# Where the last gate block gets its sigmoid: stored as exp(-x) and finished on two engines, or stored raw and finished on ScalarE

## The chip, the cores and the metric

The kernel runs on one core of one Trainium2 chip. The metric is the device time of one execution in microseconds (us). The engines of the core are TensorE (PE, with its weight loads PEld), VectorE (DVE), ScalarE (ACT), GpSimd (POOL) and SyncE (SP, which here only issues DMAs). Each engine takes its own instructions in a fixed order and waits, at the head of its queue, for whatever its next instruction needs.

## The reference

The reference is one decoder block on an input of 1024 tokens by 1024 channels, in float32. One projection gives pooling input p, queries, keys and values of four differential attention heads, and two gates of 1024 channels each. What matters here is how the two branches are merged:

```python
ya = einsum('bsc,cd->bsd', pool_mixer(p, pool_mix, pool_scale), w_branch_a)
yb = einsum('bsc,cd->bsd', diff_attention(q, k, v, ...), w_branch_b)
m = sigmoid(gate_a) * ya + sigmoid(gate_b) * yb
h = h + rms_norm(einsum('bsd,de->bse', m, w_out), mix_post_g)
```

A SwiGLU feed-forward layer follows, with silu of one product times another.

## The kernel before, in words

All activations lie in transposed form, channels on the 128 partitions and tokens along the free dimension. 1024 channels are eight blocks d of 128; 1024 tokens are two halves t of 512. A matrix product in float32 precision is made of three products of high and low parts (`triple`, lines 246 to 248); a high part is a cast on ACT, a low part a subtraction on DVE (`sub`, line 87).

The input projection runs in units. A unit computes two blocks of output columns for all tokens by a scheme of seven products (`seven_steps`). The eight gate units d = 0 to 7 compute block d of both gates; `gate_done` (line 622) is called for each finished quarter, writes it through ACT into a staging tile `g_st`, and stores the tile to DRAM (`sgd`). For d = 0 to 6 the ACT instruction is the sigmoid (line 629). The last unit, d = 7, isn't run with the others: it is kept as a generator and serves as the first part of the filler of the attention stage. For it, line 627 stores exp(-x).

The attention stage is a loop over 32 pairs of head and query block. For each pair there are scores on PE, a bias and row minimum on DVE (L771), Exp on ACT (L774), a combination of the two softmaxes on POOL (L778 to L781), transposes on PE (L797) with a cast on ACT (L799) and a subtraction on DVE to the operands `AT`, and value products on PE (L811). Between these steps PE works on a filler: the rest of the last gate unit, and then `branch(0, ...)`, the first branch (pooling output times `w_branch_a`). `PACES` says how many filler steps are written into the program for each attention step. When attention is over, `branch(1, ...)` does the second branch (attention output times `w_branch_b`), and the output projection follows, whose operands (`out_operands`) take the merged blocks in the order 0 to 7.

Both branches are one function, `branch` (line 705). It goes through 16 groups, a block d and a token half t each, of twelve matmuls (four `triple`s). `fetch` loads the weights of two blocks, four groups at a time. `gate(n)` loads the gate of group n by a DMA on SP's queue into one of two buffers for that half (named `p` for t = 0 and `sg` for t = 1 in the profile); it is called two groups ahead. `take` multiplies the group's PSUM result by the gate on DVE (`ma` in the first branch; `m` in the second, where `ma` is then added). PSUM has two banks for branch groups (`fil`), so a group needs the `take` of the group before last.

For d = 7 `gate` also finishes the sigmoid from exp(-x): POOL takes the minimum with 1e37 and adds 1 (line 726), DVE takes the reciprocal (line 727). The blocks are done in the order of line 703,

```python
BLOCKS = (0, 1, 2, 3, 6, 7, 4, 5)
```

so block 7 is groups 10 and 11 of 16 in each branch.

The framework keeps the dependencies and puts the semaphores. Outside the parts marked as manual schedule, which the attention and branch stages are not, it also decides the order of each engine's queue, from the program's order and from what it holds to be ready. On ACT a function needs its table: the compiler puts an ACT_TABLE_LOAD where the next function isn't in the table that is loaded. Copies, casts and squares have run here under each of the tables without a load.

Of the kernel before, what the change touches and what calls it, by code (L numbers as in the profile page):

```python
# [12 lines left out]
AF = mybir.ActivationFunctionType  # L13
ALU = mybir.AluOpType
# [5 lines left out]
KD = D // P  # L20
# [19 lines left out]
def block_kernel(ctx, tc, x, w_in, pool_mix, pool_scale, w_branch_a, lam_q1, lam_k1, lam_q2,  # L40
                 lam_k2, subln_g, w_branch_b, w_out, mix_pre_g, mix_post_g, ffn_pre_g, ffn_post_g,
                 w_ffn_gate, w_ffn_up, w_ffn_down, out):
    nc = tc.nc
# [24 lines left out]
    def b4(shape, dt, s):  # L68
        return sb.tile(shape, dt, tag="b4", bufs=B4, name=name(s))
# [4 lines left out]
    def fil(s):  # L74
        return ps.tile([P, HALF], F32, tag="fil", bufs=2, name=name(s))
# [13 lines left out]
    def load_w(src, k, n, s, pool=False):  # L89

        raw = wp.tile([P, k, n], F32, tag="wraw", bufs=2, name=name(s + "_raw"))
        hi = wp.tile([P, k, n], F32R, tag="whi", bufs=2, name=name(s + "_hi"))
        lo = wp.tile([P, k, n], F32R, tag="wlo", bufs=2, name=name(s + "_lo"))
        nc.sync.dma_start(raw, src.rearrange("(k p) n -> p k n", p=P))
        nc.scalar.copy(hi, raw)
        if pool:
            nc.gpsimd.tensor_tensor(out=lo, in0=raw, in1=f32(hi), op=ALU.subtract)  # L97
        else:
            sub(lo, raw, hi)
        return hi, lo  # L100
# [143 lines left out]
    def triple(o, ah, al, bh, bl, start, stop, goes_on):  # L244

        nc.tensor.matmul(o, ah, bh, start=start, stop=False, skip_group_check=goes_on)  # L246
        nc.tensor.matmul(o, ah, bl, start=False, stop=False, skip_group_check=goes_on)  # L247
        nc.tensor.matmul(o, al, bh, start=False, stop=stop, skip_group_check=goes_on)  # L248
# [12 lines left out]
    def temp(s):  # L261
        if s in ("p1", "p5", "c11"):
            return sm.tile([P, HALF], F32, tag="ft", bufs=2, name=name(s))
        return sm.tile([P, HALF], F32, tag="sg", bufs=2, name=name(s))
# [45 lines left out]
    def half(t):  # L310
        return slice(t * HALF, (t + 1) * HALF)
# [101 lines left out]
    def take(tb):  # L413
        for kq in range(2):
            nc.scalar.copy(U[f"A{tb // 4 + 1}{kq + 1}"][0][:, :, token_cols(tb)], turned[tb][kq])
            nc.scalar.copy(raw_cols(tb, kq), turned[tb][kq])
# [46 lines left out]
    with tc.manual_schedule(engines={nc.tensor.engine, nc.scalar.engine, nc.vector.engine, nc.gpsimd.engine}):  # L463
# [79 lines left out]
        for i in range(2):  # L543
            nc.vector.tensor_tensor_reduce(out=lams_at[:, 4, :], in0=lams_at[:, 2 * i, :], in1=lams_at[:, 2 * i + 1, :],
                                           scale=1.0, scalar=0.0, op0=ALU.mult, op1=ALU.add,
# [76 lines left out]
    def gate_done(d):  # L622
        st, seen = [b4([P, S], F32, "g_st") for _ in range(2)], [0, 0]

        def done(e, t, src):
            if d == KD - 1:
                nc.scalar.activation(st[e][:, half(t)], src, AF.Exp, scale=-1.0)
            else:
                nc.scalar.activation(st[e][:, half(t)], src, AF.Sigmoid)
            seen[e] += 1  # L630
            if seen[e] == 2:
                nc.scalar.dma_start(sgd[e][d], st[e])
        return done
# [66 lines left out]
            return src[k // 2][0][:, k % 2, half(t)], src[k // 2][1][:, k % 2, half(t)]  # L700
        return mov

    BLOCKS = (0, 1, 2, 3, 6, 7, 4, 5)

    def branch(e, w, mov, take):

        order = [(d, t) for d in BLOCKS for t in range(2)]
        if e == 1:
            order[:4] = [(0, 1), (1, 1), (0, 0), (1, 0)]
        ws, gates = {}, {}  # L710

        def fetch(n):
            if 2 * n < KD:
                d = BLOCKS[2 * n]
                hi, lo = load_w(w[:, d * P:(d + 2) * P], 4, 2 * P, "wb", e == 0)
                for i in range(2):
                    c = slice(i * P, (i + 1) * P)
                    ws[d + i] = hi[:, :, c], lo[:, :, c]

        def gate(n):  # L720
            if n < len(order):
                d, t = order[n]
                sg = gates[d, t] = temp(("p1", "sg")[t])
                nc.sync.dma_start(sg, sgd[e][d][:, half(t)])
                if d == KD - 1:
                    nc.gpsimd.tensor_scalar(sg, sg, 1.0e37, 1.0, op0=ALU.min, op1=ALU.add)
                    nc.vector.reciprocal(sg, sg)

        fetch(0)
        gate(0)  # L730
        gate(1)
        for n, (d, t) in enumerate(order):
            if n % 4 == 0:
                fetch(n // 4 + 1)
            gate(n + 2)
            bh, bl = ws[d]
            o = fil("branch")
            for k in range(4):
                triple(o, bh[:, k, :], bl[:, k, :], *mov(t, k), k == 0, k == 3, False)
                yield  # L740
            take(d, t, o, gates.pop((d, t)))
# [110 lines left out]
    def filling():  # L852
        yield from last_unit
        for i in range(2):
            y2.append((a8([P, 2, S], F32R, "y2h"), a8([P, 2, S], F32R, "y2l")))
            for j in range(2):
                for t, s in zip(y2[i], range(2)):
                    nc.sync.dma_start(f32(t[:, j, :]), yd[2 * i + j][:, s, :])
        ma.extend([[a8([P, 4, HALF], F32, "ma") for _ in range(KD // 4)] for _ in range(2)])
        for _ in load_head(1):  # L860
            pass
        yield from branch(0, w_branch_a, quad_mov(y2), take_a)
# [56 lines left out]
    for _ in branch(1, w_branch_b, quad_mov(OT), take_b):  # L919
        pass  # L920
# [130 lines left out]
    with tc.manual_schedule(engines={nc.tensor.engine, nc.scalar.engine, nc.vector.engine, nc.gpsimd.engine}):  # L1051
# [43 lines left out]
        for c in (c0, c1):  # L1095
            nc.vector.scalar_tensor_tensor(out=xr[:, c], in0=og[:, c], scalar=r[:, 0:1], in1=xr[:, c],
                                           op0=ALU.mult, op1=ALU.add)
# [8 lines left out]
        for c in (c0, c1):  # L1106
            nc.vector.scalar_tensor_tensor(out=og[:, c], in0=xr[:, c], scalar=r[:, 1:2], in1=gpre[:, c],
                                           op0=ALU.mult, op1=ALU.mult)
        sg = temp("sg")
# [22 lines left out]
    sg = temp("sg")  # L1132
# [185 lines left out]
```

## Time and profile before

| | us |
|---|---|
| median of 3 runs | 1276.46 |
| lowest and highest | 1275.58, 1278.18 |
| the profiled execution | 1275.52 |
| its span, first to last instruction | 1273.7 |
| last gate unit's four Exp stores (L627) | 342.8 to 354.9 |
| first branch's products with gates (`ma`) | 372.4 to 489.3 |
| second branch's products with gates (`m`) | 492.7 to 538.8 |
| table loads on ACT, four in all, each | 1.283 |

The mean granted clock of PE is 0.995 of full speed. The times in the profile's rows are microseconds from the start of the span. A row of the timeline has start, duration, engine, line, operation, output<-input and shapes, and in brackets how long the engine stood idle just before and what ended that. A row of the waits has who waited for whom, the sum, the number of waits and the longest. A row of the groups has the count, the busy sum, the mean duration in ns, and the idle time before. Matmul rows overlap: a matmul of 512 columns shows 0.39 us, but the next starts about 0.23 us later.

### The profile page before, as it was taken

Reading aid. Unit: us, or ns where it says so; the run is one execution under the profiler, and the core shown is the slowest. Engines: PE = TensorE matmul, PEld = TensorE weight load, DVE = VectorE, ACT = ScalarE, POOL = GpSimd, SP = SyncE. Lnnn points to the kernel's source line nnn. Section 1 sums busy time; section 2 is a strip of 40 time slices with the busy share of each in tenths; the row PEclk is TensorE's granted clock in tenths of the full one; section 3 lists DMA queues with packets and bytes.
Section 4 is the critical chain, followed back from the end, with each engine's and each line's share of the span. In section 5 each row is a group of like instructions: output and inputs, shape, how many; then the busy total and the mean of one; then the engine's idle time right before and its main releaser. Section 6 shows DMA issues by size and latency. Waiting matters only on the chain.

```text
span 1273.7 us, 15951 instructions
## 1 busy us (share of the span) xinstructions
PE 1244.2 (98%) x5952; PEld 1039.9 (82%) x5952; DVE 834.6 (66%) x1217; ACT 566.6 (44%) x1021; POOL 235.6 (18%) x241
## 2 busy tenths in 40 slices
PE   6999999999999899999999999999999999999997
PEld 6988778888888797788878888888888888888886
DVE  6884775435467786856699556556656537965666
ACT  7452344434567572234564333333333334454542
POOL 1000000000478871101102121022122011000221
PEclk9999999999999999999999999999999999999999
DMA  8263346234698113533315232233332358733235
GB/s 280 84 203 118 135 151 217 96 103 149 244 262 254 59 50 108 182 131 134 99 58 157 99 108 92 92 107 124 104 103 91 116 195 285 248 91 107 81 103 207
DMA packets 135566, 179.18 MB, mean 141 GB/s; under 512 B 7872, under 2 KB 90304, under 8 KB 133056
## 3 DMA queue, kind: packets, MB, share of 16 engines
q1 hardware_dynamic: 123552, 146.56, 36.8%
q10 hardware_dynamic: 11936, 31.60, 6.6%
q8 instruction: 47, 0.77, 0.3%
q14 instruction: 31, 0.25, 0.1%
HBM read 124.39 MB, written 53.74 MB: 140 GB/s over the span
## 4 chain that ended last, share of the span: by engine, by line
PE 86%; DVE 5%; ACT 3%; issue 3%; POOL 2%; DMA 1%; ACTq 0%; POOLq 0%; DVEq 0%; SPq 0%
PE Y L246 10%; PE Y L248 10%; PE Y L247 10%; PE X L246 5%; PE X L247 5%; PE X L248 5%; PE Yd L247 3%; PE Yd L248 3%; PE Yd L246 3%; PE Z L248 2%; PE Z L247 2%; PE Z L246 2%; PE o L811 2%; PE wo L972 2%; PE wo L970 2%
## 5 line engine op out<-in xcount | busy, mean ns | idle before, releaser
L164 DVE TENSOR_TENSOR p<-Z,p 128x512 f32<-128x512 f32 x35 | 24.2, 690 | 156.2 <-PE Z L248 154.5
L247 PE MATMUL Y<-A_lo,Wh 128*128 128x512 f32 x296 | 115.7, 391 | 0.3 <-DVE A_lo L87 0.3
L248 PE MATMUL Y<-A_hi,Wl 128*128 128x512 f32 x296 | 115.3, 390 | 0.1
L246 PE MATMUL Y<-A_hi,Wh 128*128 128x512 f32 x296 | 115.3, 390 | 0.0
L246 PE MATMUL Y<-S_hi,Wh 128*128 128x512 f32 x280 | 109.3, 390 | 0.0
L247 PE MATMUL Y<-S_lo,Wh 128*128 128x512 f32 x280 | 109.2, 390 | 0.0
L248 PE MATMUL Y<-S_hi,Wl 128*128 128x512 f32 x280 | 109.1, 390 | 0.0
L207 ACT CAST Wh<-wf_t 128x1024 fp32r<-128x1024 f32 x70 | 72.8, 1053 | 61.5 <-PE X L248 35.5
L87 DVE TENSOR_TENSOR Wl<-wf_t,Wh 128x1024 fp32r<-128x1024 f32 x70 | 86.9, 1248 | 13.9 <-PE Y L247 9.3
L87 DVE TENSOR_TENSOR w_op<-wd,w_op 128x512 fp32r<-128x512 f32 x77 | 56.3, 731 | 52.7 <-ACT w_op L168 52.7
L168 ACT CAST w_op<-wd 128x512 fp32r<-128x512 f32 x77 | 47.9, 622 | 73.7 <-PE Yd L248 31.6
L164 DVE TENSOR_TENSOR wf_t<-w_raw,wf_t 128x512 f32<-128x512 f32 x70 | 75.6, 1081 | 1.0
L247 PE MATMUL Yd<-w_op,s_op 128*128 128x512 f32 x176 | 68.7, 390 | 0.2 <-DVE w_op L87 0.2
L246 PE MATMUL Yd<-w_op,s_op 128*128 128x512 f32 x176 | 68.6, 390 | 0.0
L248 PE MATMUL Yd<-w_op,s_op 128*128 128x512 f32 x176 | 68.3, 389 | 0.0
L248 PEld LDWEIGHTS Y<-A_hi,Wl 128*128 128x128 f32 x296 | 55.6, 188 | 11.9 <-DVE Wl L87 0.5
L247 PEld LDWEIGHTS Y<-A_lo,Wh 128*128 128x128 f32 x296 | 55.6, 188 | 11.9 <-DVE A_lo L87 0.7
L246 PEld LDWEIGHTS Y<-A_hi,Wh 128*128 128x128 f32 x296 | 55.6, 188 | 11.6 <-ACT Wh L207 0.2
L97 POOL TENSOR_TENSOR wb_lo<-wb_raw,wb_hi 128x1024 fp32r<-128x1024 f32 x4 | 10.5, 2631 | 291.8 <-DVE Wl L87 291.8
L168 ACT CAST s_op<-s_raw 128x512 fp32r<-128x512 f32 x77 | 47.5, 617 | 34.3 <-DMA s_raw<-fsd 22.0
L246 PEld LDWEIGHTS Y<-S_hi,Wh 128*128 128x128 f32 x280 | 52.6, 188 | 12.0 <-ACT u L288 0.6
L248 PEld LDWEIGHTS Y<-S_hi,Wl 128*128 128x128 f32 x280 | 52.6, 188 | 11.0
(282 smaller groups left out, 3362.4 us busy)
## 6 DMA issues: line engine op xcount, KB each, us to landing
s_raw<-fsd SPq DMA_DIRECT2D x35, 512.0 KB, 3.8
w_raw<-in_w_in_dram SPq DMA_DIRECT2D x32, 512.0 KB, 4.2
w_raw<-in_w_ffn_gate_dram SPq DMA_DIRECT2D x22, 512.0 KB, 3.9
w_raw<-in_w_ffn_up_dram SPq DMA_DIRECT2D x22, 512.0 KB, 4.0
fsd<-fss SPq DMA_DIRECT2D x11, 1024.0 KB, 3.9
wd<-in_w_ffn_down_dram SPq DMA_DIRECT2D x44, 256.0 KB, 5.3
fsd<-F SPq DMA_DIRECT2D x33, 256.0 KB, 2.1
qkd<-qk_st ACTq DMA_DIRECT2D x16, 512.0 KB, 3.9
```

The lines of the kernel that those rows point to most:

```text
L87: nc.vector.tensor_tensor(out=o, in0=a, in1=f32(hi), op=ALU.subtract)
L97: nc.gpsimd.tensor_tensor(out=lo, in0=raw, in1=f32(hi), op=ALU.subtract)
L164: nc.vector.tensor_tensor(out=o, in0=a, in1=b, op=op)
L168: nc.scalar.copy(hi, a)
L207: nc.scalar.copy(hi, a)
L246: nc.tensor.matmul(o, ah, bh, start=start, stop=False, skip_group_check=goes_on)
L247: nc.tensor.matmul(o, ah, bl, start=False, stop=False, skip_group_check=goes_on)
L248: nc.tensor.matmul(o, al, bh, start=False, stop=stop, skip_group_check=goes_on)
L811: nc.tensor.matmul(o, ats[b // 4][:, j, b % 4 * P:(b % 4 + 1) * P], V[:, b, :, :], start=b == 0 and j == 0, stop=b == qb and j == 1)
L970: nc.tensor.matmul(o[e], mh[:, k, :], wh, start=k == 0, stop=False)
L972: nc.tensor.matmul(o[e], ml[:, k, :], wh, start=False, stop=k == KD - 1)
```

## The change

Line 627 becomes a plain copy: block 7 of both gates is stored without a function. `gate` only loads. A new step, `prepare(n + 1)`, is called one group ahead and puts a sigmoid on ACT, in place, for the gates of block 7. The list of blocks goes away; both branches take the blocks in the order 0 to 7, so that block 7 is groups 14 and 15.

```diff
         def done(e, t, src):
             if d == KD - 1:
-                nc.scalar.activation(st[e][:, half(t)], src, AF.Exp, scale=-1.0)
+                nc.scalar.copy(st[e][:, half(t)], src)
             else:
                 nc.scalar.activation(st[e][:, half(t)], src, AF.Sigmoid)
...
-    BLOCKS = (0, 1, 2, 3, 6, 7, 4, 5)
-
     def branch(e, w, mov, take):
 
-        order = [(d, t) for d in BLOCKS for t in range(2)]
+        order = [(d, t) for d in range(KD) for t in range(2)]
...
         def fetch(n):
             if 2 * n < KD:
-                d = BLOCKS[2 * n]
+                d = 2 * n
...
                 nc.sync.dma_start(sg, sgd[e][d][:, half(t)])
-                if d == KD - 1:
-                    nc.gpsimd.tensor_scalar(sg, sg, 1.0e37, 1.0, op0=ALU.min, op1=ALU.add)
-                    nc.vector.reciprocal(sg, sg)
+
+        def prepare(n):
+            if n < len(order) and order[n][0] == KD - 1:
+                sg = gates[order[n]]
+                nc.scalar.activation(sg, sg, AF.Sigmoid)
...
             gate(n + 2)
+            prepare(n + 1)
             bh, bl = ws[d]
```

## The prediction

> **What bounds the kernel now.** I read the page's busy times first, then the list of who waited for whom on TensorE (PE) around the part that the diff touches, then busy times by stretch, then the timeline at the two places that the waits point to.
>
> ```profile
> span 1273.7 us, 15951 instructions
> PE 1244.2 (98%) x5952; PEld 1039.9 (82%) x5952; DVE 834.6 (66%) x1217; ACT 566.6 (44%) x1021; POOL 235.6 (18%) x241
> ```
>
> PE is the bound: 98% of the span. A change can win only where PE stands still or runs at a lower clock, and it can lose only by making PE stand still. The diff touches the attention stage with its filler (the first branch, about 355 to 489 us) and the second branch (489 to 538 us). From 340 to 545 us PE waited for other engines at these places, the two longest of four:
>
> ```profile
> PE aT L797 <- DVE AT L87: 4.2, 1, 4.2
> PE branch L246 <- DVE m L164: 2.9, 1, 2.9
> ```
>
> Each is one wait. The stretches around them (columns: stretch and its length; PE, weight loads, DVE, ACT, POOL busy with the number of instructions; granted clock of PE; DMA share; GB/s):
>
> ```profile
> 415.00:432.00 17.00, 16.97 (x104) 14.86 (x102) 10.30 (x24) 10.36 (x30) 15.96 (x16) 1.00 0.20 66
> 432.00:436.40 4.40, 0.22 (x2) 0.05 (x1) 3.79 (x4) 0.00 (x0) 4.04 (x5) 0.95 0.31 108
> 436.40:440.00 3.60, 3.60 (x13) 3.12 (x14) 2.71 (x8) 2.67 (x8) 2.23 (x4) 0.58 0.00 0
> 455.00:470.00 15.00, 15.00 (x100) 13.29 (x99) 12.69 (x28) 11.04 (x30) 12.72 (x14) 1.00 0.22 69
> 470.00:489.60 19.60, 18.78 (x126) 16.33 (x126) 13.02 (x37) 12.11 (x42) 7.88 (x13) 1.00 0.12 41
> 517.00:520.00 3.00, 0.10 (x1) 0.00 (x0) 3.00 (x3) 1.04 (x1) 1.05 (x1) 1.00 0.08 30
> 520.00:526.00 6.00, 5.97 (x18) 4.38 (x19) 5.88 (x6) 0.00 (x0) 0.00 (x0) 0.72 0.21 72
> ```
>
> PE does nothing from 432.0 to 436.4 and from 517 to 520, and after each gap its clock is down for a few us: 0.58 over 3.6 us, 0.72 over 6 us. Elsewhere it is full. What stands in the way is seen on POOL and DVE, first gap:
>
> ```profile
> 430.63 1.94 POOL L726 TENSOR_SCALAR p<-p 128x512 f32<-128x512 f32 x1
> 432.93 1.92 POOL L726 TENSOR_SCALAR sg<-sg 128x512 f32<-128x512 f32 x1
> ...
> 432.61 3.35 DVE L727 RECIPROCAL p<-p 128x512 f32<-128x512 f32 x1 [4.68 <-POOL p L726]
> 435.88 0.36 DVE L87 TENSOR_TENSOR AT<-aT,AT 128x256 fp32r<-128x256 f32 x1
> ...
> 436.38 1.51 PE L797 MATMUL aT<-ident,E 128*128 128x128 f32 x6 [4.18 <-DVE AT L87]
> ```
>
> The reciprocal of a block-7 gate stands at the head of DVE's queue. DVE idles 4.68 us until POOL has done the minimum and the addition, computes for 3.35 us, and only then comes to the low-half subtraction that frees the PSUM bank of the next transposes. In the second branch the same:
>
> ```profile
> 513.76 2.28 POOL L726 TENSOR_SCALAR p<-p 128x512 f32<-128x512 f32 x1 [25.33 <-DMA p<-sgd]
> ...
> 516.08 3.35 DVE L727 RECIPROCAL p<-p 128x512 f32<-128x512 f32 x1 [1.82 <-POOL p L726]
> 519.35 0.63 DVE L164 TENSOR_TENSOR m<-branch,p 128x512 f32<-128x512 f32 x1
> ...
> 520.03 0.50 PE L246 MATMUL branch<-OTh,wb_hi 128*128 128x512 f32 x1 [2.93 <-DVE m L164]
> ```
>
> The product at 519.35 empties the PSUM bank that the group after next needs, and it stood behind the reciprocal.
>
> **What is removed.** In each branch two POOL operations and two reciprocals:
>
> ```profile
> L727 DVE RECIPROCAL p<-p 128x512 f32<-128x512 f32 x2 | 6.7, 3352 | 6.5 <-POOL p L726 6.5
> L727 DVE RECIPROCAL sg<-sg 128x512 f32<-128x512 f32 x2 | 6.7, 3344 | 0.0
> ```
>
> That is 13.4 us of DVE and 4 x about 2 us of POOL, but only what PE felt counts. The first of each pair made PE wait; behind the other two no PE wait of this size is listed. So the gain is 4.18 + 2.93 = 7.11 us of waiting, and the clock lost after it: 3.60 x (1 - 0.58) = 1.51 and 6.00 x (1 - 0.72) = 1.68, together 3.19. Sum 10.30 us. I count all of it because from 440 to 470 and after 526 PE is busy without a break: work that comes earlier stays earlier.
>
> **What is changed at no price.** The last unit's four gate evacuations stay four ScalarE instructions of about the same length (Exp against copy):
>
> ```profile
> L627 ACT ACTIVATE g_st<-p x2: 615/624/632, 342.8 to 348.4; 128x512 f32<-128x512 f32 x2
> ...
> 335.17 0.59 ACT L285 COPY p<-X 128x512 f32<-128x512 f32 x1 [1.39 <-PE X L248]
> 335.77 1.28 ACT L774 ACT_TABLE_LOAD   x1
> 337.07 1.15 ACT L774 ACTIVATE E<-E,nm 128x1024 f32<-128x1024 f32 x1
> ```
>
> The load of the Exp table at 335.77 belongs to the attention's own Exp (L774), so it stays. The order of blocks changes which gate and weight columns are loaded when; the number, size and queue (SP) of the DMAs are the same, and a buffer still comes free two groups of the same half earlier. The output projection reads the merged blocks in the order 0 to 7, so the block that comes last now is also the one that it needs last: nothing lost there.
>
> **What is added: four sigmoids and their tables.** One sigmoid of a gate is this long, by the other units:
>
> ```profile
> L629 ACT ACTIVATE g_st<-u x7: 625/632/636, 212.6 to 327.6; 128x512 f32<-128x512 f32 x7
> ```
>
> Each waits for its gate's DMA, and behind it in ScalarE's queue stand the AT casts (PE's value products need them), the O copies and the Exps. A sigmoid between Exps also needs a table load before it and one after it: 1.28 us each, the next instruction starting 1.30 us after the load did. So the price depends on where in the queue the two sigmoids of the first branch stand. In program order they come after the last Exp: by the paces of the interleaving, the first of them is written after the last scores. But the queues are not filled in program order:
>
> ```profile
> 457.03 0.81 ACT L774 ACTIVATE E<-E,nm 128x640 f32<-128x640 f32 x1
> ...
> 459.05 1.06 ACT L95 CAST wb_hi<-wb_raw 128x1024 fp32r<-128x1024 f32 x1 [0.15 <-PE branch L247]
> ...
> 478.25 0.40 ACT L774 ACTIVATE E<-E,nm 128x128 f32<-128x128 f32 x1 [0.28 <-DVE nm L771]
> ```
>
> The cast at 459.05 prepares the second branch's first weights, which the program writes after the whole attention, and it ran 19 us before the last Exp, as soon as its buffer was free. The sigmoids will be taken as early if their gates are there. The last two gate loads of the first branch, their landing time, and the products that use them:
>
> ```profile
> 453.75 0.32 SPq L724 DMA_DIRECT2D p<-sgd  x1
> 460.36 0.32 SPq L724 DMA_DIRECT2D sg<-sgd  x1
> ...
> p<-sgd SPq DMA_DIRECT2D x3, 256.0 KB, 2.7
> ...
> 486.59 0.69 DVE L164 TENSOR_TENSOR ma<-branch,p 128x512 f32<-128x512 f32 x1 [0.33 <-PE branch L248]
> 489.32 0.69 DVE L164 TENSOR_TENSOR ma<-branch,sg 128x512 f32<-128x512 f32 x1 [0.16 <-PE branch L248]
> ```
>
> In the times of before, the gates are there at 456.5 and 463.1, with Exps at 457 and until 478 around them. So I expect both sigmoids between Exps, each with its own pair of loads: 4 x 1.28 + 2 x 0.63 = 6.38 us more for ScalarE between about 456 and 470. There it is busy for 11.04 of 15 us, 3.96 us free. The bill is thus bounded by nothing (it falls into gaps, PE fills with branch products) and by all 6.38 us plus the two slow clocks that such gaps were followed by, 2 x 1.5, together 9.4 us. I take the overrun, 6.38 - 3.96 = 2.42 us, since that stretch is where the sigmoids will stand; later ScalarE has 7.5 us free before 489.6. A gain from the added work itself is excluded, since it removes no wait. As the change is, a rule stands against it. The Trainium skill ("ScalarE: Activation LUTs", section "Table sets: the hidden batching unit") advises grouping activations by table set, and in "What ACT_TABLE_LOAD costs" it prices a switch at 1283 ns plus about 1380 ns of drain. Here the load itself agrees and the drain isn't seen: the load at 335.77 follows the copy's end at once. With the page's drain the four loads would cost 5.5 us more and the run would come to about 1274.1 us.
>
> In the second branch no Exp follows, so there is one load for both sigmoids, or none if the last one stays. The gate before last is asked for and used there at
>
> ```profile
> 525.21 0.32 SPq L724 DMA_DIRECT2D p<-sgd  x1
> ...
> 536.63 0.68 DVE L164 TENSOR_TENSOR m<-branch,p 128x512 f32<-128x512 f32 x1
> ```
>
> which leaves 11.4 us for a landing of about 3, a load and 0.63 us: free. What hides it is ScalarE's idleness; even if late, the two last products free banks that PE doesn't wait for at once.
>
> **Sum.** The profiled execution took 1275.52 us (span 1273.7), 0.94 below the median of the three runs, 1276.46. 1275.52 - 10.30 + 2.42 = 1267.64 us, and on the scale of the median 1268.6 us.
>
> **Rivals.**
>
> *The sigmoids stand after the last Exp* (program order holds). One extra load in the first branch, in a stretch with 7.5 us of ScalarE free. For it: the program text; against it: the cast at 459.05. 1276.46 - 10.30 = 1266.2 us.
>
> *All of the tables' time reaches PE.* Two hold-ups of ScalarE by 2 x 1.28 + 0.63 = 3.19 us, each through the AT casts, each with a slow clock behind: 9.4 us, which gives 1275.6 us, no change to measure. For it: PE's order is fixed, and a late cast stops it. Against it: PE has branch products to run between, and the Exps run four blocks ahead.
>
> *The wait moves to POOL.* POOL is busy for 15.96 of 17 us before the first gap and its scaling of E comes before PE's transposes. If it is late next, the 4.18 us come back: 1272.8 us. Against it: 3.9 us of what POOL did from 430 to 435 is what goes away.
>
> *Slower: a sigmoid at the head of ScalarE's queue waits for its gate.* The queue would be fixed for a landing of about 2.7 us; landings reach 9.9 us:
>
> ```profile
> DMA to landing us min/median/max: 2.5/3.0/9.9
> ```
>
> 7.2 us more each, 14.4 for both, with the 6.38 and less the 3.96 free: 16.8 us, so 1276.46 - 10.30 + 16.8 = 1283.0 us. It decides from 10.3 us of exposed waiting, some 5 per sigmoid. Against it: DMA is at 0.22 of its share there and the loads of that stretch land in 2.7 us.
>
> **How the numbers follow.** Sigmoids between Exps with an overrun of about 2.4 us: 0.47. After the Exps: 0.23. Wait moved to POOL: 0.08. All exposed: 0.12. Gate waits: 0.10. The predicted time is the first, 1268.6 us. A measurement of this kernel can tell about 0.2% (2.6 us) from no change, so the first three are faster (0.78), all exposed is the same (0.12), the last slower (0.10). The range goes from the best case, 1266.2, less the 1.7 us by which the runs of before scatter upward from their median, 1264.5, to the upper bound of the table cost, 1275.6; it leaves out the last rival.
>
> **What would show it.** L726 and L727 are gone, the PE waits of 4.2 and 2.9 us with them, and the granted clock is 1.00 through both places. ScalarE shows four sigmoids in the branches and five more table loads (one in the rival with program order); PE's waits for AT casts in the first branch's last third should sum to about 2.4 us. Wrong it is if those waits pass 10 us, if the wait for DVE at the transposes stays, or if PE's new gaps bring the slow clock again.

## The result and the profile after

The changed kernel took 1265.35 us (median of four runs, 1264.89 to 1266.26) against 1276.46 before; the ratio is 0.9912 with a 95% interval of 0.9892 to 0.9931. That is inside the range, near its lower end of 1264.5, and 3.3 us better than the predicted 1268.6. Two executions were slow ones and are left out of all medians: one of the kernel before (2095 us) and one of a run below (1783 us, at a granted clock of 0.656). The profiled execution has a span of 1263.0 us, 10.7 less than before:

```profile
span 1263.0 us, 15954 instructions
PE 1240.5 (98%) x5952; PEld 1037.5 (82%) x5952; DVE 822.2 (65%) x1213; ACT 574.2 (45%) x1030; POOL 226.6 (18%) x237
```

DVE has lost 12.4 us and POOL 9, ScalarE has gained 7.6; PE has the same instructions and is busy for 3.7 us less; a matmul at a low clock counts as busy, so this is about the part of the gain that was slow clock (3.19 us in the sum). All of PE's waits for other engines between 340 and 545 us:

```profile
PE oT L846 <- DVE O L833: 1.1, 2, 0.8
PE s L768 <- DVE nm L772: 0.3, 1, 0.3
```

The waits of 4.2 and 2.9 us behind the reciprocals are gone. The stretches at the two old gaps, and below them the two in which the sigmoids now stand and what follows (columns as before: PE, PEld, DVE, ACT, POOL, clock, DMA share, GB/s):

```profile
432.00:436.40 4.40, 4.40 (x25) 3.85 (x24) 3.64 (x8) 2.88 (x8) 4.13 (x6) 1.00 0.30 101
436.40:440.00 3.60, 3.60 (x26) 3.33 (x26) 3.28 (x6) 3.04 (x10) 2.57 (x5) 1.00 0.24 77
...
517.00:520.00 3.00, 3.00 (x15) 2.49 (x14) 2.46 (x6) 2.27 (x5) 0.00 (x0) 1.00 0.99 343
520.00:526.00 6.00, 6.00 (x28) 4.95 (x28) 5.29 (x8) 4.25 (x5) 0.00 (x0) 1.00 0.77 272
...
455.00:470.00 15.00, 15.00 (x106) 13.59 (x106) 10.75 (x24) 14.88 (x33) 6.33 (x9) 1.00 0.22 65
470.00:484.00 14.00, 12.87 (x77) 10.57 (x75) 8.79 (x26) 7.74 (x29) 5.22 (x9) 1.00 0.14 46
```

PE is busy throughout at full clock where it stood. From 455 to 470 ScalarE is full, 14.88 of 15 us, and PE doesn't notice in that stretch: 15.00 of 15. ScalarE's queue there, with the loads and what they serve, and below it the second branch:

```profile
455.03 1.24 ACT L848 ACTIVATE OTh<-oT,sgc 128x512 fp32r<-128x512 f32 x2
456.29 1.28 ACT L727 ACT_TABLE_LOAD   x1
457.59 0.63 ACT L727 ACTIVATE p<-p 128x512 f32<-128x512 f32 x1
...
458.88 1.28 ACT L775 ACT_TABLE_LOAD   x1
460.18 0.62 ACT L775 ACTIVATE E<-E,nm 128x384 f32<-128x384 f32 x1
...
465.52 0.22 ACT L775 ACTIVATION_READ_ACCUMULATOR E<-E,nm 128x1 f32 x1
465.76 1.28 ACT L727 ACT_TABLE_LOAD   x1
467.06 0.63 ACT L727 ACTIVATE sg<-sg 128x512 f32<-128x512 f32 x1
467.71 1.28 ACT L775 ACT_TABLE_LOAD   x1
469.00 0.51 ACT L775 ACTIVATE E<-E,nm 128x256 f32<-128x256 f32 x1
...
519.80 1.28 ACT L727 ACT_TABLE_LOAD   x1
...
522.58 0.62 ACT L727 ACTIVATE sg<-sg 128x512 f32<-128x512 f32 x1
```

Both sigmoids stand between Exps, each with a load before it and one after it, as forecast; a fifth load at 519.80 serves the second branch. Where the time went by stage is read from the first and last start of the second branch's products and of the output projection's, before and then after:

```profile
L246 PE MATMUL branch<-OTh,wb_hi x64: 389/389/633, 489.6 to 537.6; 128*128 128x512 f32 x64
L970 PE MATMUL wo<-woh,mh x128: 389/389/476, 538.3 to 630.9; 128*128 128x512 f32 x128
...
L246 PE MATMUL branch<-OTh,wb_hi x64: 389/389/474, 484.4 to 527.3; 128*128 128x512 f32 x64
L971 PE MATMUL wo<-woh,mh x128: 389/389/476, 528.0 to 620.6; 128*128 128x512 f32 x128
```

The first matmul of the second branch moved from 489.6 to 484.4 us and the first of the output projection from 538.3 to 528.0. So the first branch gave 5.2 us, the second 5.1, and everything else the remaining 0.4.

### The profile page after: what moved, and what is told of

Its sections match the earlier page's. It is cut to its first block, busy times and chain, and to the rows that moved or that the text cites. A ratio compares the mean times of both kernels' runs of the same rounds, so it can differ in the third digit from the quotient of the medians.

```text
span 1263.0 us, 15954 instructions
## 1 busy us (share of the span) xinstructions
PE 1240.5 (98%) x5952; PEld 1037.5 (82%) x5952; DVE 822.2 (65%) x1213; ACT 574.2 (45%) x1030; POOL 226.6 (18%) x237
## 4 chain that ended last, share of the span: by engine, by line
PE 87%; DVE 5%; ACT 3%; issue 2%; POOL 1%; DMA 0%; ACTq 0%; DVEq 0%; SPq 0%; POOLq 0%
PE Y L246 10%; PE Y L248 10%; PE Y L247 10%; PE X L246 5%; PE X L247 5%; PE X L248 5%; PE Yd L247 3%; PE Yd L248 3%; PE Yd L246 3%; PE o L812 3%; PE Z L248 2%; PE Z L247 2%; PE Z L246 2%; PE branch L248 2%; PE branch L247 2%
```

## The experiments

My theory: the gain is the two waits behind the reciprocals, with the slow clock after each, and the table loads cost little. Rivals: the order of blocks makes the gain; a reciprocal on DVE is enough to make the waits, whatever POOL does; the loads do cost 2.4 us and the removed waits were worth more.

**The order alone.**

```diff
-    BLOCKS = (0, 1, 2, 3, 6, 7, 4, 5)
+    BLOCKS = (0, 1, 2, 3, 4, 5, 6, 7)
```

> The kernel before with the natural order of blocks alone; block 7 still stored as exp(-x) and finished on POOL and DVE. My theory (the gain is the two waits behind the reciprocals with the slow clock after them): the first branch keeps a wait of PE behind a reciprocal, now near its end; in the second branch block 7 is last, no later group needs its PSUM bank, so the 2.9 us wait and the 1.7 us of slow clock after it go: about 1271.8 us (1270 to 1274). Rival, the order makes the whole gain: about 1265.3 us. Rival, the order does nothing: 1276.5 us.

Measured: 1269.04 us (1268.8 to 1269.93), ratio 0.9941 (0.9926 to 0.9956). PE's longest waits:

```profile
PE aT L797 <- DVE AT L87: 1.3, 1, 1.3
PE oT L845 <- DVE O L832: 1.1, 2, 0.7
PE branch L246 <- DVE m L164: 0.8, 1, 0.8
```

This is between theory and rival and fits neither number: the order alone brings some 7.5 us, by the ratio. The theory had the first branch's wait survive at full length and the second's vanish; in fact both shrank, to 1.3 and 0.8 us, and in the stretches around them (466 to 480 and 524 to 532 us) the granted clock stayed at 1.00. All four reciprocals are still there. The two before which DVE still waited for POOL, of the first and of the second branch:

```profile
473.27 3.35 DVE L727 RECIPROCAL sg<-sg 128x512 f32<-128x512 f32 x1 [1.51 <-POOL sg L726]
524.39 3.35 DVE L727 RECIPROCAL p<-p 128x512 f32<-128x512 f32 x1 [0.28 <-POOL p L726]
```

DVE waited 1.51 and 0.28 us, where it had waited 4.68 and 1.82. Against 1264.4 us for the best kernel below, the same operations on POOL and DVE cost some 12 us in one place of the stream and under 5 in another.

**The sigmoid alone**, in the order of before: the changed kernel with `BLOCKS` put back.

> The sigmoid on ScalarE alone, with the order of blocks of before (block 7 as groups 10 and 11 of 16). My theory: both waits go, the tables are hidden here too: 1265.3 us, within 1 us. Rival, the order makes the gain or hides the tables: 1268 us or more, with PE waiting for casts on ScalarE near 430 us.

Measured: 1267.74 us (1267.39 to 1268.01), ratio 0.9929 (0.9914 to 0.9944). Both old waits are gone, but it is 2.4 us slower than the changed kernel. The waits that are left:

```profile
PE oT L848 <- DVE O L835: 1.7, 2, 0.9
PE s L770 <- DVE nm L774: 0.5, 2, 0.3
PE oT L848 <- DVE nm L774: 0.5, 1, 0.5
```

My figure missed. Either the order costs by itself or the loads cost more in that place (here the first branch's stand from 426.67 to 434.59 us); the tanh kernels below tell these apart.

**Minimum and addition on DVE instead of POOL**, kernel before otherwise.

```diff
-                    nc.gpsimd.tensor_scalar(sg, sg, 1.0e37, 1.0, op0=ALU.min, op1=ALU.add)
+                    nc.vector.tensor_scalar(sg, sg, 1.0e37, 1.0, op0=ALU.min, op1=ALU.add)
```

> The kernel before, but minimum and addition run on DVE too, just ahead of the reciprocal, instead of on POOL. It tells the wait for POOL (DVE idle 4.68 and 1.82 us) from the reciprocal's own 3.35 us. My theory, the chain through two engines makes the waits: the first of PE's waits nearly goes, of the second (2.93 - 1.82 + about 0.65) some 1.8 us stay: about 1268.5 us (1266.5 to 1271). Rival, a reciprocal of 3.35 us on DVE is enough: about 1275 us.

> Minimum and addition on DVE again, for its profile: 1268.9 us within 1, with the first of PE's two waits (4.2 us behind the reciprocal) gone or under 1 us, and 1.5 to 2.5 us left of the second.

Measured: 1268.84 us (1267.57 to 1268.95), and 1268.87 us (1268.17 to 1269.56) the second time, ratio 0.9936 (0.9919 to 0.9953). The second run's DVE at the first place, PE's two longest waits, and the stretch of the second place:

```profile
428.33 0.62 DVE L726 TENSOR_SCALAR p<-p 128x512 f32<-128x512 f32 x1
428.99 3.35 DVE L727 RECIPROCAL p<-p 128x512 f32<-128x512 f32 x1
```

```profile
PE branch L246 <- DVE m L164: 1.2, 2, 0.9
PE aT L797 <- DVE O L164: 0.9, 1, 0.9
```

```profile
505.00:520.00 15.00, 13.86 (x60) 10.73 (x58) 13.13 (x14) 3.88 (x5) 0.00 (x0) 1.00 0.44 141
```

One engine does both steps in 4.0 us with nothing in between, where the pair of engines held DVE for 4.68 + 3.35. The 4.2 us wait is gone, though the reciprocal is there and as long as ever. The rival "a reciprocal is enough" falls: the wait came mostly from DVE standing behind POOL. What is left are short waits, at a clock of 1.00; the second place has two that sum to 1.2 us, less than the 1.5 to 2.5 expected. The run is still 4.5 us behind the best kernel below.

**Only the second branch's gates raw, with the sigmoid.**

```diff
-            if d == KD - 1:
-                nc.scalar.activation(st[e][:, half(t)], src, AF.Exp, scale=-1.0)
+            if d == KD - 1 and e == 1:
+                nc.scalar.copy(st[e][:, half(t)], src)
+            elif d == KD - 1:
+                nc.scalar.activation(st[e][:, half(t)], src, AF.Exp, scale=-1.0)
...
-                if d == KD - 1:
+                if d == KD - 1 and e == 0:
...
+        def prepare(n):
+            if e == 1 and n < len(order) and order[n][0] == KD - 1:
+                sg = gates[order[n]]
+                nc.scalar.activation(sg, sg, AF.Sigmoid)
...
             gate(n + 2)
+            prepare(n + 1)
```

> Order of before; raw storing and the sigmoid for the second branch's gates alone, POOL and DVE finish those of the first. My theory: 2.93 us of wait and 1.68 us of slow clock go, the wait at 432 us and its slow clock stay: 1276.5 - 4.6 = 1271.9 us. Rival, the gain is mostly the first branch's (DVE and POOL relief in attention): 1274.5 us or more.

Measured: 1271.68 us (1271.2 to 1272.8), ratio 0.9959 (0.9945 to 0.9973). The first wait stands as it was, with its slow clock:

```profile
PE aT L805 <- DVE AT L87: 4.2, 1, 4.2
```

```profile
432.00:436.40 4.40, 0.24 (x2) 0.00 (x0) 3.73 (x3) 0.00 (x0) 4.04 (x5) 0.91 0.33 107
436.40:440.00 3.60, 3.55 (x12) 3.10 (x13) 2.60 (x7) 2.67 (x8) 2.25 (x4) 0.50 0.00 0
```

As the theory had it, 1271.9, and not the rival's 1274.5 or more: of the two places the second is worth 4.8 us against the 1276.46 of the result, or 5.4 against the 1277.07 that the kernel before took on this run's chip.

**What the loads cost.** Three kernels beside the changed one on the same chip. The first copies instead of taking the sigmoid (block 7's gates are used without their function); the second reaches the sigmoid as 0.5 + 0.5 tanh(x/2):

```diff
-                nc.scalar.activation(sg, sg, AF.Sigmoid)
+                nc.scalar.copy(sg, sg)
```

```diff
-                nc.scalar.copy(st[e][:, half(t)], src)
+                nc.scalar.activation(st[e][:, half(t)], src, AF.Tanh, scale=0.5)
...
-                nc.scalar.activation(sg, sg, AF.Sigmoid)
+                nc.scalar.activation(sg, sg, AF.Copy, bias=0.5, scale=0.5)
```

> The changed kernel once more, as the measure for the next three on the same chip: 1265.3 us, within 0.8.

> The changed kernel with a copy in place of each of the four sigmoids: the function of block 7's gates is left out, so the five table loads go and the four instructions stay. My theory, after the result: the loads are hidden, so no more than 0.6 us less than the changed kernel. Rival, the overrun of 2.4 us that the prediction charged is there, and the removed waits were worth more than 10.3: about 2.4 us less, 1262.9.

> The same result without a table switch: the last unit stores tanh(x/2), and ScalarE finishes with a copy of scale 0.5 and bias 0.5 instead of the sigmoid. No extra table load is in its program. If the loads are hidden: the time of the changed kernel within 0.6 us. If they cost 2.4 us: 1262.9 us.

Measured: the changed kernel 1265.39 us (1264.95 to 1266.08); with copies 1264.03 (1263.80 to 1264.43); with tanh 1264.54 (1264.14 to 1264.99), ratios to before 0.9912 (0.9898 to 0.9926), 0.9902 (0.9886 to 0.9917), 0.9905 (0.9891 to 0.9918). So the five loads cost 1.4 us by the first, 0.9 by the second: more than my 0.6, less than the rival's 2.4. Neither theory's number held. The kernel with copies has ScalarE and PE so:

```profile
455.00:470.00 15.00, 15.00 (x113) 14.12 (x112) 11.96 (x31) 12.62 (x37) 9.17 (x13) 1.00 0.18 54
470.00:484.00 14.00, 13.47 (x76) 10.93 (x75) 7.90 (x19) 5.85 (x21) 3.05 (x5) 1.00 0.16 58
```

```profile
PE oT L846 <- DVE O L833: 0.2, 1, 0.2
```

Without loads ScalarE has 12.62 us of work there instead of 14.88, and 5.85 instead of 7.74 in the next stretch, where PE is busy for 13.47 of 14 us instead of 12.87. The loads pushed attention work later, and its end, where the last heads are transposed, had to be waited for: 1.1 us against 0.2.

**More loads**: blocks 4 to 7 stored raw, `d >= KD - 4` in `gate_done` and the same in `prepare`; then the same with tanh.

> The suspected cost made larger: blocks 4 to 7 are stored raw, and their 16 gates get the sigmoid in the branches, most of those in the first branch between Exps with two table loads each. If loads between Exps are hidden: 1265.3 to 1267 us. If each pair costs PE 1.2 us or more (the prediction's 2.4 us for two): some five more pairs, 1271 us or more.

> Blocks 4 to 7 as tanh(x/2), finished in the branches by 16 scaled copies on ScalarE: the instructions of the run with 16 sigmoids without its table loads. If the loads made that run 7.4 us slower than the changed kernel: 1264.5 to 1266 us. If the 16 instructions in place did: about 1272 us.

Measured with sigmoids: 1272.75 us (1272.19 to 1273.02), ratio 0.9969 (0.9956 to 0.9981). With tanh: 1264.19 us (1263.91 to 1264.59), ratio 0.9901 (0.9887 to 0.9916). The sigmoid kernel's loads (groups: count, busy, mean ns; one of the sixteen is the attention's own), its stretches before the end of attention, PE's longest wait, and the last product of the first branch ahead of that wait:

```profile
L775 ACT ACT_TABLE_LOAD x8 | 10.3, 1283 | 0.1
L727 ACT ACT_TABLE_LOAD x8 | 10.3, 1283 | 0.1
```

```profile
424.00:464.00 40.00, 40.00 (x221) 34.40 (x220) 22.96 (x50) 39.65 (x74) 25.57 (x29) 1.00 0.20 63
464.00:468.00 4.00, 2.45 (x17) 1.79 (x16) 2.61 (x6) 3.99 (x8) 1.73 (x3) 1.00 0.15 45
468.00:476.00 8.00, 5.79 (x31) 5.12 (x32) 5.89 (x11) 5.37 (x13) 6.24 (x5) 0.79 0.50 158
```

```profile
PE oT L846 <- DVE nm L772: 3.2, 1, 3.2
...
465.51 0.40 PE L248 MATMUL branch<-y2h,wb_lo 128*128 128x512 f32 x1
```

The same stretches with tanh:

```profile
424.00:464.00 40.00, 40.00 (x260) 35.80 (x260) 32.56 (x73) 34.28 (x92) 34.57 (x40) 1.00 0.13 41
464.00:468.00 4.00, 4.00 (x32) 3.74 (x31) 3.15 (x6) 3.05 (x8) 2.86 (x4) 1.00 0.55 163
468.00:476.00 8.00, 7.47 (x51) 6.07 (x50) 5.30 (x18) 5.06 (x19) 2.67 (x5) 1.00 0.15 53
```

Ten loads more than in the changed kernel, 12.8 us of ScalarE, cost 7.4 us, as the second of the two expectations had it; the sixteen finishing instructions without loads cost nothing. From 424 to 464 ScalarE is full, 39.65 of 40 us, and PE isn't touched: attention falls behind, and PE takes products of the first branch in its place. Their last one is at 465.51, where the changed kernel has it at 483.21. Then there is nothing left to fill with: PE stands for 3.2 us, and from 468 to 476 its clock is 0.79. So a full ScalarE cost PE nothing as long as filler was left, and was paid for when the filler was used up. (What released that one wait was DVE, which came to it behind two subtractions of 1.2 us for the next weights, at 466.56 and 467.76; how much of the 7.4 us is this order in DVE's queue wasn't tested.)

**The order once more, without loads**: the tanh kernel with `BLOCKS` put back.

> The kernel with tanh(x/2) stored and no extra table load, once more, as the measure for the other runs on this chip: 1264.5 us, within 0.8.

> The tanh kernel with the order of blocks of before (block 7 as groups 10 and 11). The sigmoid with that order took 1267.7 us, 2.4 more than with the natural order. If the order matters only through table loads that fall on a busier ScalarE: within 0.8 us of the natural order, 1264.5. If the order itself costs, whatever finishes the gates: about 1267 us.

Measured: 1264.38 us (1264.20 to 1264.66) with the natural order, 1264.62 us (1264.47 to 1264.76) with that of before. The order by itself is worth nothing that shows once nobody waits for POOL. With the order of before the sigmoid and its loads cost 3.1 us (1267.74 against 1264.62, on different chips, and the same by the ratios 0.9929 and 0.9905), with the natural order 0.9 to 1.4: the 2.4 us that the sigmoid kernel lost were the loads in an earlier place. Why they cost more there wasn't traced. The best versions are those with tanh: 1264.4 us, and 1264.2 with four blocks, against 1265.4 for the change.

## Why the prediction was right

**Where the time stood.** Right. Two waits of PE behind the reciprocals and the slow clock after each made the gain; by stage it is 5.2 and 5.1 us, where the sum had 4.18 + 1.51 and 2.93 + 1.68. The run with the second branch alone gave 4.8 to 5.4 us for the second term of 4.61. That DVE stood behind POOL, as the prediction read it, is most of the two waits: the run with minimum and addition on DVE and the run with the order alone each bring some 8 of the 12 us with every reciprocal in place. The reciprocals themselves account for at most the 4.5 us that those two runs still lack to the best kernel.

**Its size.** Undersized. Without the loads the gain is 1276.4 - 1264.0 = 12.3 us by medians, not 10.30, and 1273.7 - 1262.0 = 11.7 by spans. The kernel with copies has its stages so:

```profile
L246 PE MATMUL branch<-OTh,wb_hi x64: 389/389/474, 483.4 to 526.3; 128*128 128x512 f32 x64
L971 PE MATMUL wo<-woh,mh x128: 389/389/477, 527.0 to 619.7; 128*128 128x512 f32 x128
```

So the first branch gave 6.2 us where the sum had 5.69, the second 5.1 where it had 4.61, and 0.4 came behind them. Part of this can be read: the idle time in brackets counts from the modelled end of the last matmul (516.71 + 0.39), but the next one was due 0.23 us after its start, so each gap is about 0.16 us longer than its row says. The rest of the 1.4 us wasn't traced to a row. By medians there is more, since the profiled execution of before was one of its fastest, 1275.52 in runs from 1275.22 to 1278.71; the forecast was shifted by the same 0.94 us, as if every run had the same gaps.

**The table loads.** The place was right (between Exps, ready as soon as the gate had landed, against the program's order), and so was the count of five. The step that failed in size is the overrun: 2.42 us charged, 0.9 to 1.4 measured. Its path was wrong too. The sign named for it, waits of PE for AT casts that sum to 2.4 us, isn't there: the list of waits above has none. ScalarE was full, but PE ran branch products meanwhile, and only the part that reached the end of attention was felt, as 1.1 us at the transposes of O against 0.2 without loads. Here the overrun of a stretch was more than its price. The Trainium skill's price of a switch ("ScalarE: Activation LUTs", section "What ACT_TABLE_LOAD costs": the load plus a drain of about the same length) isn't borne out: the instruction ahead ends at 456.27, the load runs from 456.29 to 457.57, and the sigmoid starts at 457.59. Its rule to group activations by table set (section "Table sets: the hidden batching unit") is, by the run with sixteen gates: fifteen loads more than with tanh, and 8.6 us.

**The rivals.** The sigmoids did not move behind the last Exp. The wait didn't move to POOL: POOL is as busy as before from 432 to 436 us and PE is at 4.40 of 4.40. No sigmoid stood long at the head of the queue for its gate: the gaps before it and before its load in the queue above are under 0.1 us. "All of the tables' time reaches PE" is wrong for four loads, but the run with fourteen between Exps goes that way. "The sigmoids stand after the last Exp" gave 1266.2 us, nearer to the measured 1265.35 than the chosen 1268.6, with a mechanism that didn't happen; that its number fits better is chance. The two errors of the chosen sum point the same way: by the run with copies the gain was too small by 2.0 us and the charge too large by 1.1, which is nearly all of its 3.3 us.

**The second branch.** Right: its one load and two sigmoids, from 519.80 to 523.2 us, stand in a stretch in which PE is busy without a break (6.00 of 6 us from 520 to 526).

## What to carry to other kernels

Read what stands at the head of an in-order queue: a long instruction whose input comes from another engine blocks everything behind it for that engine's time too, and moving both steps to one engine took most of that wait away here, the finishing on an engine with slack all of it. Price a gap of PE of about 3 us or more with the slow clock that follows it. Ask how much filler PE has left before calling added work on another engine free. Between Exps, look for a function that lives in Exp's table (tanh for sigmoid) before paying for table loads.

## What the runs showed of the hardware that I had not expected

Waits of PE of 0.7 to 1.3 us (order alone, DVE alone) left the granted clock at 1.00, while those of 2.9 and 4.2 us were followed by 0.72 and 0.50 to 0.58 for a few us (with only the second branch changed, 0.69 for four us more), and the 3.2 us of the run with sixteen sigmoids by 0.79 over 8 us. The slow clock need not start with the first matmul behind the gap: in the second branch of before, PE stood until 520.03, the matmuls from 520.37 to 521.29 still started 0.23 us apart, and only those behind them 0.40 us and more. With the long gaps went some of the spread of the runs: 1275.2 to 1278.7 us in 27 runs before, 1264.9 to 1266.3 in 8 after, 1264.1 to 1265.0 in 8 with tanh. Minimum and addition of 128x512 took 0.41 to 0.62 us on DVE and 1.92 to 2.28 us on POOL. Tanh ran without a table load between Exps, and, for blocks 4 to 6, after the sigmoids of the units before, under their table.
